# The last four stores behind the If for both paths, and another order of quarter products at the end

## The chip, the cores and the metric

One NeuronCore of one Trainium2 chip runs the kernel; the other cores are idle. The metric is the device time of the core, in microseconds (us). A core has five engines that run beside each other: TensorE (PE, with its weight loads shown as PEld), VectorE (DVE), ScalarE (ACT), GpSimd (POOL) and SyncE (SP, which computes nothing here and issues transfers). Each works through its own list of instructions in order; semaphores tie them together.

## The reference

```python
m, k, n = 4096, 4096, 4096
a = np.random.randn(m, k).astype(np.float32)
b = np.random.randn(k, n).astype(np.float32)
alpha = np.float32(0.01)

def reference(a, b, alpha):
    x = np.matmul(a, b)
    return np.where(x > 0, x, alpha * x)
```

A product of two 4096 x 4096 matrices with a leaky ReLU behind it, in float32.

## The kernel before

The output is cut into regions of 1024 x 1024: group `g` of rows (4) by column block `j` (4). A region is four blocks of 512 x 512, and a block is held as four row tiles `mt` of 128 rows by 512 columns. All inputs are rounded to float16 on the way in. Past the first region a region is computed by seven products of half-size matrices in place of eight, with sums of blocks of A (`s1` to `s4`) and of B made beforehand by VectorE. `product` (line 788) runs a whole product, 128 x 512 per matmul. In the regions of the last groups three of the seven, the fourth, the sixth and the seventh, are themselves split into seven products of quarters: `quarter_product` (line 738) multiplies a 256 x 1024 quarter of the A side by a 1024 x 256 quarter of the B side, in 16 matmuls of 128 x 256 (8 chunks `c` of the depth by 2 row tiles `m`). In it `x[h, k]` and `b[k, n]` are quarters themselves, `sx(n)` are sums of quarters of A that were kept in memory and are loaded again, and `t(n)` are sums of quarters of B.

Each product of quarters enters one or more quarters of the block. With rows `r` (row tiles 0 and 1, or 2 and 3) and columns `n` (left or right 256), the seven enter as follows: `x[0,0] b[0,0]` into all four; `x[0,1] b[1,0]` into (0,0); `sx(2) t(2)` into (0,1), (1,0) and (1,1); `sx(1) t(1)` into (0,1) and (1,1); `sx(4) b[1,1]` into (0,1); `sx(3) b[0,1]` into (1,0) and (1,1); `x[1,1] t(4)` into (1,0).

The last region's seventh product is written out by itself, in `seventh_at_the_end`. Its block already has a part in the PSUM banks `y[0..3]` (one per row tile). The banks `one` and `one_more` (their left halves are `ones`) collect what enters several quarters, the bank `other` holds `sx(1) t(1)`, and `kept[mt]` in SBUF, four tiles of 128 x 512 float32, collects the block. ScalarE copies banks to `kept`, VectorE adds banks to it (`add`, line 949; lines 928, 929 and 940) and applies `leaky` (line 310). With `by_row=True` a product finishes its first row tile before it begins the second. `leave` (line 960) applies `leaky` to a pair of row tiles and issues their stores on SP.

The instructions of this part stand in the order in which they are written: the kernel runs under a manual schedule, and each engine gets its own in that order.

The shortened product holds only for inputs of a certain evenness. Sums over the squares of A and B are collected beside the work; `judge` makes them into one number `good`, and `values_load` reads it into a register `even` of every engine. Behind the last region all engines compare `even`: where it is 1, SP issues the last store (line 1201); where it is not, the `Else` computes everything again in bfloat16 with plain products, 8 row blocks by 8 column blocks, and stores it over the whole output. With the inputs above `even` is 1. At the end of either path each engine brings the semaphore counts that belong to it up to what the other path would have left, and goes to the close of the program (line 1262): SP waits for each DMA counter, and the engines meet twice.

SP's list at the end, in order: four stores of `v_pairs`, four of `u2_pairs`, the load of `even`, the two stores of row tiles 0 and 1 (line 960), the store of row tile 2 (line 944), the branch (line 1200), the store of row tile 3 (line 1201). Each store is 256 KB.

## Time and profile before

| | us |
|---|---|
| median of 3 runs | 1539.24 (1538.66 to 1540.42) |
| the profiled execution, its own time | 1540.23 |
| its span | 1538.1 |
| PE busy in the span | 1524.4 (99%) |
| DVE, ACT, POOL busy | 1158.1, 426.0, 281.9 |
| end of the last matmul, of the last VectorE instruction | 1528.85, 1530.83 |
| issue of the last store | 1530.90 |

The span runs from the first to the last instruction that the profiler recorded, 2.1 us less than the execution's own time. The profile page gives busy time per engine, the chain of work that ended last, groups of instructions, waits and transfers; a line such as L738 is a line of the kernel's source, and a "q" behind an engine's name (SPq) marks an instruction of that engine's sequencer, which issues, waits or branches and leaves the engine's data path idle. A row of a source line gives the operation, its count, its least, median and greatest length in ns, and its first and last start in us. TensorE's granted clock was 0.998 of full speed.

### The profile page before, as it was taken

What the parts mean: (1) busy time and instruction counts of PE and PEld (TensorE: products, weight loads), DVE (VectorE), ACT (ScalarE), POOL (GpSimd) and SP (SyncE); (2) the same over time, 40 slices, a digit from 0 to 9 for tenths busy, and PEclk for the clock granted to TensorE, in tenths of its full rate; (3) what the DMA queues carried; (4) which work ended last, traced back from release to release, by engine and by line L of the source; (5) the groups of instructions that cost most, each with busy time, mean ns of one, the idle gap of its engine ahead of it and who ended that gap; (6) DMA issues with size and microseconds to landing.
All of it is one profiled execution on the core that took longest, in us unless ns stands there. A gap on an engine that the chain in (4) does not pass through costs nothing.

```text
span 1538.1 us, 21821 instructions
## 1 busy us (share of the span) xinstructions
PE 1524.4 (99%) x8667; PEld 846.8 (55%) x8667; DVE 1158.1 (75%) x1201; ACT 426.0 (28%) x730; POOL 281.9 (18%) x458
## 2 busy tenths in 40 slices
PE   9999999999999999999999999999999999999997
PEld 4444444444446567574544747557544475747656
DVE  4368867766699686768769698676977868797496
ACT  2201334647310213103641130312454112041210
POOL 5641110243202011022220202010331110101100
PEclk9999999999999999999999999999999999999999
DMA  9999895998879979599797979969899895948924
GB/s 247 187 212 202 235 282 168 174 192 182 229 277 282 252 174 275 135 291 258 171 290 263 287 183 213 253 160 320 165 245 309 216 282 144 292 164 182 286 99 140
DMA packets 205442, 342.87 MB, mean 223 GB/s; under 512 B 18833, under 2 KB 148113, under 8 KB 195346
## 3 DMA queue, kind: packets, MB, share of 16 engines
q0 software_dynamic: 136704, 129.00, 52.7%
q1 hardware_dynamic: 62002, 186.81, 32.9%
q10 hardware_dynamic: 6624, 25.56, 4.4%
q8 instruction: 70, 1.15, 0.3%
q14 instruction: 42, 0.34, 0.1%
HBM read 361.76 MB, written 106.43 MB: 304 GB/s over the span
## 4 chain that ended last, share of the span: by engine, by line
PE 67%; DVE 1%; issue 0%; DVEq 0%
PE ps L788 45%; PE ps L738 22%; DVE c L310 0%; DVE c L949 0%; DVE c L843 0%; DVE c L940 0%; DVE c L954 0%; DVE b L667 0%; DVEq L940 0%
## 5 line engine op out<-in xcount | busy, mean ns | idle before, releaser
L788 PE MATMUL ps<-b,a 128*128 128x512 f16 x2624 | 570.8, 379 | 0.0
L788 PE MATMUL ps<-b,s 128*128 128x512 f16 x2240 | 489.2, 379 | 0.0
L788 PEld LDWEIGHTS <-a 128*128 128x128 f16 x2624 | 256.6, 98 | 307.9 <-issue 0.3
L788 PEld LDWEIGHTS <-s 128*128 128x128 f16 x2240 | 219.1, 98 | 262.6 <-issue 0.4
L575 DVE TENSOR_TENSOR b<-b 128x4096 f16<-128x4096 f16 x104 | 235.1, 2289 | 65.4 <-DMA b<-in_b_dram 56.7
L519 POOL DMA_DIRECT2D b<-in_b_dram x160 | 118.6, 746 | 866.2 <-PE ps L738 327.6
L801 ACT COPY c<-ps 128x512 f32<-128x512 f32 x164 | 84.6, 596 | 452.1 <-PE ps L788 365.0
L141 DVE STREAM_TRANSPOSE a<-a 128x512 uint32<-128x512 uint32 (+2 forms) x120 | 126.8, 1104 | 96.6 <-DMA a<-in_a_dram 96.6
L132 POOL DMA_DIRECT2D a<-in_a_dram x252 | 137.3, 551 | 264.8 <-ACT junk L594 97.6
L738 PEld LDWEIGHTS <-q 128*128 128x128 f16 x1424 | 139.3, 98 | 16.9 <-issue 0.8
L594 ACT ACTIVATE junk<-a 128x512 bf16<-128x512 f16 x192 | 121.1, 631 | 97.6 <-DMA a<-in_a_dram 92.4
L310 DVE SCALAR_TENSOR_TENSOR c<-c 128x1024 f32<-128x1024 f32 (+1 forms) x121 | 141.5, 1212 | 4.4 <-ACT c L801 4.2
L230 ACT ACTIVATE sq<-b 128x2048 bf16<-128x2048 f16 x64 | 119.1, 1909 | 57.6 <-DVE sq L239 41.8
L738 PEld LDWEIGHTS <-a 128*128 128x128 f16 x1200 | 117.3, 98 | 17.9 <-DVE q L677 0.3
L949 DVE TENSOR_TENSOR c<-ps,c 128x512 f32<-128x512 f32 x142 | 88.8, 683 | 48.0 <-PE ps L788 34.4
L282 PE MATMUL ps<-b,a 128*128 128x512 f16 x512 | 112.8, 379 | 2.1 <-DVE part L321 0.9
L738 PE MATMUL ps<-b,q 128*128 128x256 f16 x784 | 92.1, 273 | 0.6 <-DVE c L843 0.6
L738 PE MATMUL ps<-b,a 128*128 128x256 f16 x752 | 88.3, 273 | 0.0
L282 PEld LDWEIGHTS <-a 128*128 128x128 f16 x512 | 49.7, 98 | 63.1 <-issue 3.2
L890 ACT COPY c<-ps 128x512 f32<-128x512 f32 x9 | 5.3, 586 | 269.9 <-PE ps L738 120.2
L738 PEld LDWEIGHTS <-s 128*128 128x128 f16 x624 | 61.0, 98 | 7.1
L843 DVE TENSOR_TENSOR c<-ps,c 128x512 f32<-128x512 f32 x80 | 52.3, 687 | 13.5 <-PE ps L738 13.5
(104 smaller groups left out, 903.7 us busy)
## 6 DMA issues: line engine op xcount, KB each, us to landing
b<-in_b_dram POOLq DMA_DIRECT2D x168, 512.0 KB, 13.0
out_dram<-c SPq DMA_DIRECT2D x240, 256.0 KB, 5.6
a<-in_a_dram POOLq DMA_DIRECT2D x244, 128.0 KB, 5.6
b<-kept SPq DMA_DIRECT2D x20, 1024.0 KB, 9.1
q<-kept_qs ACTq DMA_DIRECT2D x40, 512.0 KB, 7.7
s<-kept_s SPq DMA_DIRECT2D x18, 1024.0 KB, 7.5
q<-kept_qa SPq DMA_DIRECT2D x28, 512.0 KB, 6.7
b<-kept_last SPq DMA_DIRECT2D x12, 1024.0 KB, 11.5
```

Source lines behind the costliest of these rows:

```text
L132: nc.gpsimd.dma_start(a16[32 * q:32 * q + 32], src.rearrange("(g i) w -> i g w", i=32))
L141: nc.vector.transpose(part.rearrange("p c m e -> p c (m e)").bitcast(U32) .rearrange("p c (g i) -> p g c i", i=32), src[:, :, i * n:(i + 1 ...
L230: nc.scalar.activation(to, self.parts[n], SQUARE)
L282: nc.tensor.matmul(ps, a_cols(at[0, h, u], c, mt, (h, u) == (0, 0)), bt[0, u, nt][:, c, :], start=first, stop=last,)
L310: nc.vector.scalar_tensor_tensor(t, t, alpha, t, op0=MULT, op1=MAX if alpha <= 1 else MIN)
L519: nc.gpsimd.dma_start(t[:, c:c + 4, :], b_rows(j, u, c, 4, nt, g > 0))
L575: nc.vector.tensor_tensor(f(to), f(x0), f(x1), op)
L594: nc.scalar.activation(junk, piece[:, q, :], SQUARE, accum_out=to[:, 4 * n + q:4 * n + q + 1])
L738: nc.tensor.matmul(to[m], xq[:, c // 2, rows, c % 2], yq[:, c, :], start=first and c == 0 and m < banks, stop=c == KC - 1, skip_group_chec ...
L788: nc.tensor.matmul(banks[mt], a_cols(t, c, mt, t is first_a), B(half, nt, k)[:, c, :], start=first and (k, c) == todo[0], stop=(k, c) == t ...
L801: nc.scalar.copy(kept[mt], banks[mt])
L949: nc.vector.tensor_add(to, bank, to)
```

## The change

Two things change. In `seventh_at_the_end` the seven products of quarters stand in another order, the block is finished quarter by quarter, and no store is issued in it: it returns the four pairs of destination and tile. Behind the last region the `If` now holds the fallback alone, with the condition turned round, and has no `Else`; the four stores stand behind it, for both paths. So that they store the right thing on either path, the fallback does not store the four tiles of this block itself: it writes them to a buffer `back` in memory and loads them from there, on POOL's queue, into the tiles `last[mt][1]`, which the stores then write out.

The order of products before: `x[0,0] b[0,0]`, `sx(4) b[1,1]`, `sx(2) t(2)`, `sx(1) t(1)`, `x[0,1] b[1,0]`, `x[1,1] t(4)`, `sx(3) b[0,1]`. After: `x[0,0] b[0,0]`, `x[0,1] b[1,0]`, `sx(2) t(2)`, `sx(1) t(1)`, `sx(4) b[1,1]`, `sx(3) b[0,1]`, `x[1,1] t(4)`, the last two by row. `even` is now loaded behind the second product, before it was behind the fifth.

```diff
+            part = lambda t, n: t[:, n * HALF:(n + 1) * HALF]
+            onto = lambda r, n: [part(y[2 * r + m], n) for m in range(2)]
+            ones = [part(bank, 0) for bank in (one, one_more)]
+
+            def more(mt, n, bank):
+                nc.vector.tensor_add(part(kept[mt], n), bank, part(kept[mt], n))
 
             quarter_product(x[0, 0], b[0, 0], ones, True, banks=2)
-            copies(0)
+            for m in range(2):
+                nc.scalar.copy(part(kept[m], 0), ones[m])
+            for mt in (2, 3):
+                nc.scalar.copy(part(kept[mt], 1), part(y[mt], 1))
+            quarter_product(x[0, 1], b[1, 0], onto(0, 0))
+            for mt in range(2):
+                more(mt, 0, part(y[mt], 0))
+            leaky(block(0, 0))
+            even = nc.values_load(good[0:1, 0:1], min_val=0, max_val=1)
+            quarter_product(sx(2), t(2), ones)
+            for m in range(2):
+                nc.scalar.copy(part(kept[m], 1), ones[m])
+            quarter_product(sx(1), t(1), into(other), True)
+            for r in (1, 0):
+                nc.vector.tensor_add(block(r, 1), pair(other), block(r, 1))
             quarter_product(sx(4), b[1, 1], onto(0, 1))
-            quarter_product(sx(2), t(2), ones)
-            copies(1)
+            for mt in range(2):
+                more(mt, 1, part(y[mt], 1))
+            leaky(block(0, 1))
+            quarter_product(sx(3), b[0, 1], ones, by_row=True)
+            for m in range(2):
+                nc.scalar.copy(part(kept[2 + m], 0), ones[m])
+                more(2 + m, 1, ones[m])
+            leaky(block(1, 1))
+            quarter_product(x[1, 1], t(4), onto(1, 0), by_row=True)
             for mt in (2, 3):
-                nc.scalar.copy(kept[mt][:, HALF:], y[mt][:, HALF:])
-            quarter_product(sx(1), t(1), into(other), True)
-            nc.vector.tensor_add(block(0, 1), pair(other), block(0, 1))
-            nc.vector.tensor_add(block(1, 1), pair(other), block(1, 1))
-            quarter_product(x[0, 1], b[1, 0], onto(0, 0))
-            even = nc.values_load(good[0:1, 0:1], min_val=0, max_val=1)
-            add(kept[:2], y[:2])
-            leave(pairs[:1], 0, 1)
-            quarter_product(x[1, 1], t(4), onto(1, 0))
-            for mt in (2, 3):
-                nc.scalar.copy(kept[mt][:, :HALF], y[mt][:, :HALF])
-            quarter_product(sx(3), b[0, 1], ones, by_row=True)
-            for mt in (2, 3):
-                both_halves = kept[mt].rearrange("p (h n) -> p h n", h=2)
-                nc.vector.tensor_add(both_halves, ones[mt - 2].unsqueeze(1).to_broadcast([P, 2, HALF]), both_halves)
-                leaky(kept[mt])
-                last = place(g, 0, mt, j, 1), kept[mt]
-                if mt == 2:
-                    nc.sync.dma_start(*last)
-            return even, last
+                more(mt, 0, part(y[mt], 0))
+                leaky(part(kept[mt], 0))
+            return even, [(place(g, 0, mt, j, 1), kept[mt]) for mt in range(MT)]
...
-    with tc.If(even == 1) as inputs:
-        nc.sync.dma_start(*last)
-
-    with inputs.Else():
+    back = dram_pool.tile([MT, P, NT], FP32, name="back")
+    about_to_leave = 2 * regions[-1][0], 2 * regions[-1][1] + 1
+    with tc.If(even == 0):
...
-                    nc.sync.dma_start(out[(m * MT + mt) * P:(m * MT + mt + 1) * P, cols], t)
+                    if (m, n) == about_to_leave:
+                        nc.sync.dma_start(back[mt], t)
+                        nc.gpsimd.dma_start(last[mt][1], back[mt])
+                    else:
+                        nc.sync.dma_start(out[(m * MT + mt) * P:(m * MT + mt + 1) * P, cols], t)
+    for to, t in last:
+        nc.sync.dma_start(to, t)
```

More of the change, by code (lines that the diff above doesn't have):

```diff
@@ L912, in seventh_at_the_end @@
             block = lambda r, n: pairs[r][:, :, n * HALF:(n + 1) * HALF]
-            onto = lambda r, n: [y[2 * r + m][:, n * HALF:(n + 1) * HALF] for m in range(2)]
-            ones = [bank[:, :HALF] for bank in (one, one_more)]
-            def copies(n):
-                for m in range(2):
-                    nc.scalar.copy(kept[m][:, n * HALF:(n + 1) * HALF], ones[m])
-            quarter_product(x[0, 0], b[0, 0], ones, True, banks=2)
-            copies(0)
-            quarter_product(sx(4), b[1, 1], onto(0, 1))
```

## The prediction

> **What bounds the kernel now.** I read the page first (shares, then the chain that ended last), next the timeline of the last 35 us, and then the sequencers' own rows of the lines that hold the branch and the close. From the page:

> ```profile
> span 1538.1 us, 21821 instructions
> PE 1524.4 (99%) x8667; PEld 846.8 (55%) x8667; DVE 1158.1 (75%) x1201; ACT 426.0 (28%) x730; POOL 281.9 (18%) x458
> ```

> TensorE is busy for 1524.4 of 1538.1 us, and the change leaves its 8667 matmuls as they are. What can move is what lies around them: 13.7 us, nearly all of it at the end. The chain that ended last, from 1440 us on, in order of time (start, length, what):

> ```profile
> 1504.40 23.59 PE ps L738 x216
> ...
> 1528.08 0.70 DVE c L940
> ...
> 1530.14 0.69 DVE c L310
> ```

> It passes from TensorE to VectorE 0.8 us before the last matmul ends (1526.94 + 1.91 = 1528.85) and stops at 1530.83: 7.3 us of the span come after all arithmetic. The timeline of that end:

> ```profile
> 1526.61 1.23 DVE L310 SCALAR_TENSOR_TENSOR c<-c 128x1024 f32<-128x1024 f32 x1
> 1526.94 1.91 PE L738 MATMUL ps<-b,q 128*128 128x256 f16 x16
> 1528.08 0.69 DVE L940 TENSOR_TENSOR c<-ps,c 128x512 f32<-128x512 f32 x1 [0.25 <-PE ps L738]
> 1528.81 0.69 DVE L310 SCALAR_TENSOR_TENSOR c<-c 128x512 f32<-128x512 f32 x1
> 1529.42 0.68 DVE L940 TENSOR_TENSOR c<-ps,c 128x512 f32<-128x512 f32 x1
> 1529.57 0.33 SPq L944 DMA_DIRECT2D out_dram<-c  x1
> 1530.14 0.69 DVE L310 SCALAR_TENSOR_TENSOR c<-c 128x512 f32<-128x512 f32 x1
> 1530.90 0.33 SPq L1201 DMA_DIRECT2D out_dram<-c  x1
> ```

> Two adds and two leaky ReLUs, each 512 wide, follow the last product one behind the other; the last store is issued 0.07 us later. The other 7.2 us are in the views of line 1200 (the If) and line 1262 (the program's close):

> ```profile
> L1200 SPq EVENT_SEMAPHORE  x7: 17/17/17, 1533.4 to 1533.8; - x7
> L1200 PEldq COMPARE_BRANCH  x2: 90/2090/4089, 1526.7 to 1529.1; - x2
> L1200 SPq COMPARE_BRANCH  x2: 43/46/49, 1529.9 to 1533.9; - x2
> L1200 DVEq COMPARE_BRANCH  x2: 51/53/55, 1530.2 to 1531.0; - x2
> ```

> ```profile
> L1262 SPq EVENT_SEMAPHORE  x14: 17/28/28, 1536.5 to 1538.1; - x14
> ...
> L1262 DVEq DRAIN  x2: 10/34/58, 1534.3 to 1537.6; - x2
> ```

> SP sits still until 1533.4, when row tile 2's store (issued 1529.57, landing 3.8) is in; it then brings seven DMA counters up to what the other path would have left (1533.4 to 1533.9), branches over the fallback at 1533.9, and shows nothing until the first closing wait at 1536.5. None of its closing waits lasts over 0.028 us, so those 2.6 us are no wait for a transfer. VectorE loses 1531.0 to 1534.3 = 3.3 in the same place, PE 4.1, ACT 1527.8 to 1530.2 = 2.4, POOL 1506.6 to 1509.2 = 2.6. I read this as the code of the jump's target coming in: the DMA records show instruction blocks of 8 KB moving at 1534.8 and 1534.9.

> [...]

> **The change, part by part.**

> 1. TensorE: the same seven products of 16 matmuls in another order, 0. In the built order the products wait for nothing that is not there: `sx(2)`, `sx(1)` and `t(2)` keep their slots (third, fourth), `sx(4)` and `t(4)` move later, and `sx(3)`, whose load is issued at 1514.9 (such loads land in 7.7, the median over the run), is used at 1525.4, not 1527.1. New waits: `sx(4)`'s product onto `y[0..1]` waits for VectorE's adds of the left halves, done by 1521.5, two slots before. If this cover failed it would cost what is late, one for one.

> 2. VectorE: nine instructions become fifteen, narrower. Widths: 512 takes 0.69 and 1024 takes 1.22, so 256 takes about 0.42 (an estimate on that line; bounds 0.34, half of 0.69, and 0.69). Independent ones start 0.08 before the one ahead ends, dependent ones 0.03 after. With products ending each 1.745 us up to 1528.85, I walk the queue: left halves of tiles 0 and 1 and their leaky 1520.7 to 1522.2 (the queue is free at 1520.8); the two adds of `other` 1523.65 to 1524.9; right halves of tiles 0, 1 1525.3 to 1526.0, leaky to 1526.8; tile 2 right at 1526.7, tile 3 right at 1527.6 (it stands behind ScalarE's copy, 0.38 from 1527.1), leaky of both to 1528.7; then tile 2 left 1528.6 to 1529.05, leaky to 1529.5; tile 3 left to 1529.85, leaky to 1530.3. So VectorE ends at 1530.3, not 1530.83: 0.5 gained, not the 1.1 that the short last steps alone would give, because the wide leaky of tiles 2 and 3 now stands ahead of them. Bounds 0.2 to 0.9.

> 3. The If: every engine now jumps over the fallback before the stores. SP's comparison moves up to about 1522.9, right behind its load of `even` (issued at 1521.7, the last register step at 1522.8); no store stands before it. Jump 2.5 to 4.1: 1525.4 to 1527.0. At the far side it waits for all eight counters (the stores in flight landed by 1523.8) and raises them, eight steps at 0.07: 1526.0 to 1527.6. Queued behind it are the four stores. Tile 0 and 1 are ready at 1526.8, tile 2 at 1529.5, tile 3 at 1530.3, so the jump on SP costs nothing: 2.7 us or more of slack up to the third store, and up to 4.1 the first two only go out later. The stores also wait for counters that POOL raises; POOL jumps at 1505.4. The adjacent branches behind the jump I take at 0: at the program's start the same kind of branch leaves no row, and 0.07 us separate the instructions on its two sides.

> 4. The tail. Last store issued 1530.35. Its landing: rows give 2.3 to 3.8 near the end (2.0 is the least since 1500); in the run before the last 2 KB packets end by 1533.6, 2.7 after its issue. I take 2.65: 1533.0. Then SP's closing waits: twelve in 1536.5 to 1537.2, 0.06 each; the last store's counter is sixth, six are left, 0.4, drains 0.1, and the handshake of all engines, 1537.3 to 1538.1, 0.8. Sum 1533.0 + 1.3 = 1534.3.

> 5. VectorE's own jump is on the way too: it leaves at 1529.9, as its last leaky is issued; with its own 3.3 it is at its drain at 1533.35, just ahead of SP at 1533.5. With 2.5 it has 0.9 to spare; with PE's 4.1 it sets the end at 1535.0. PE leaves at 1526.8 and is back by 1530.9.

> Sum: 1538.1 - 1534.3 = 3.8 gained: 0.5 from VectorE, 0.5 the counters, 2.6 the jump, 0.3 closing waits passed while the last store is in flight, 0.1 lost between landings. The profiled run took 1540.23, 2.1 around its span; the median of the runs, 1539.24, lies 0.99 lower. I set the difference against the median: **1535.4 us**.

> **Rivals.**

> One, a new wait takes the jump's place: VectorE's fetch takes PE's 4.1 (1535.0), or the last store takes row tile 2's 3.8 (1530.35 + 3.8 + 1.3 = 1535.45), as both now fall into the same microseconds. Gain 2.7 to 3.1: 1536.4. For it: the slow rows are those beside stores. Against: there the last store still took 2.7.

> Two, the gap was no code: SP's 2.6 us come anyway at the close. Left are 0.5 + 0.5 + 0.3 = 1.3: 1537.9. [...] Against: five engines show the gap, each right behind its second branch, POOL 29 us before the end.

> Three, the change does not do what it says: the jump leaves the tail of one engine and is paid several times by another. The path not taken has three branches (into the stub, behind the If, to the close). If each fetches anew, VectorE needs three times 2.5 to 3.3 from 1529.9: 1537.4 to 1539.8, plus drain and handshake 0.9: 1538.3 to 1540.7, middle 1539.5, or **1540.6 us, slower**. It decides once VectorE is back later than 1537.2. Against: the branch at the start without a gap. SP would stand at 1534.8 by 4.0 a hop, and its stores with it, so slower by over 0.2% lies inside this case.

> **How the numbers follow.** Forecast 0.66, rival one 0.16, two 0.08, three 0.08, other 0.02. The likeliest case's range: landing 2.0 to 3.2, VectorE's width and its jump, and half a microsecond of the runs' scatter (1538.66 to 1540.42): 1534.3 to 1536.3. With rival one and the lower edge of two: 1534.2 to 1537.4. 0.2% (3.1 us, to 1536.2 and 1542.3) is about what can be told from no change. Faster: five sixths of the forecast and a third of rival one, 0.60. Slower by that much: a good half of rival three and mishaps, 0.06. Within: the rest, 0.34.

> **What would show it.** SP's branch near 1522.9 and nothing between the last store's issue and its closing wait but the landing; the last leaky 256 wide, ending near 1530.3; the close within 1.5 us of the landing; VectorE's drain before SP's. It is wrong if a gap of 2 us or more stands behind the landing, if TensorE idles between the last seven products, or if VectorE or PE reports after SP.

## The result, and the profile after

| | before | changed |
|---|---|---|
| median, us | 1539.89 (22 runs, 1537.35 to 1544.40) | 1537.31 (22 runs, 1535.30 to 1538.92) |
| span of the profiled execution | 1538.1 | 1535.5 |
| last product ends | 1528.85 | 1528.79 |
| last VectorE instruction ends | 1530.83 | 1530.22 |
| last store issued | 1530.90 | 1530.25 |
| span's end behind the last product | 9.27 | 6.75 |

The ratio of the times is 0.9980, 95% interval 0.9973 to 0.9987: faster by about 3 us (the medians lie 2.6 apart), less than the 3.8 forecast. A second set of 11 runs beside other experiments gave 0.9978 (0.9969 to 0.9987). The last row is the one to compare between profiles. The beginning of the last seven products wanders between 1514.5 and 1516.7 from one profile to the next, in kernels that are the same up to there, and the span wanders with it.

The end of the chain that ended last, in the changed kernel (start, length, what):

```profile
1504.34 22.72 PE ps L738 x208
...
1527.08 0.38 ACT c L943
...
1527.48 0.44 DVE c L919
...
1529.80 0.43 DVE c L310
```

It leaves TensorE at 1527.1, earlier than before: from there a copy on ScalarE and then VectorE's queue, not the last product, set the end of the arithmetic. The rows of the If's line (1209), of the four stores' line (1243, the last line of its view) and of the close (1274):

```profile
L1209 SPq EVENT_SEMAPHORE  x8: 17/17/17, 1525.5 to 1526.1; - x8
...
L1209 SPq COMPARE_BRANCH  x1: 50/50/50, 1522.8 to 1522.8; - x1
L1209 PEldq COMPARE_BRANCH  x1: 3731/3731/3731, 1526.7 to 1526.7; - x1
...
L1209 DVEq EVENT_SEMAPHORE  x1: 21/21/21, 1533.2 to 1533.2; - x1
```

```profile
DMA to landing us min/median/max: 2.4/3.8/3.9
```

```profile
L1274 DVEq DRAIN  x2: 10/14/17, 1533.3 to 1535.0; - x2
```

SP branches at 1522.8, is back after 2.7, and has raised its counters by 1526.1, before the first tile is ready. TensorE's jump takes 3.7 from 1526.7, VectorE's 3.4 from 1529.8; both report before SP. Behind the last landing no jump is left. The landings in the line of 1243 are those of the first three stores (3.8, 3.9 and 2.4); that of the last is not among them. The new length is in SP's waits, from 1520 us on (who waited for what, sum, times, longest):

```profile
SPq L1274 <- DMA out_dram<-c: 3.3, 2, 2.3
...
SPq L1209 <- SPq L1209: 2.7, 1, 2.7
```

SP now waits 2.3 us for the last store alone. That store was issued at 1530.25, and SP's wait for its counter ends at 1534.22: 3.97, where the sum had 2.65.

### The profile page after: what moved, and what is told of

The parts are those of the page before. It is cut to its first block, busy times and chain, and to the rows that moved or that the text cites. A ratio compares the mean times of both kernels' runs of the same rounds, so it can differ in the third digit from the quotient of the medians.

```text
span 1535.5 us, 21822 instructions
## 1 busy us (share of the span) xinstructions
PE 1523.8 (99%) x8667; PEld 846.9 (55%) x8667; DVE 1158.7 (75%) x1207; ACT 426.2 (28%) x730; POOL 281.9 (18%) x458
## 3 DMA queue, kind: packets, MB, share of 16 engines
q8 instruction: 70, 1.15, 0.3%
## 5 line engine op out<-in xcount | busy, mean ns | idle before, releaser
L738 PEld LDWEIGHTS <-q 128*128 128x128 f16 x1424 | 139.3, 98 | 16.2
L310 DVE SCALAR_TENSOR_TENSOR c<-c 128x1024 f32<-128x1024 f32 (+2 forms) x123 | 141.5, 1190 | 4.5 <-ACT c L801 4.2
L738 PEld LDWEIGHTS <-a 128*128 128x128 f16 x1200 | 117.4, 98 | 18.4 <-DVE q L677 0.8
L738 PE MATMUL ps<-b,q 128*128 128x256 f16 x784 | 91.8, 273 | 0.0
L738 PE MATMUL ps<-b,a 128*128 128x256 f16 x752 | 88.3, 273 | 0.0
L738 PEld LDWEIGHTS <-s 128*128 128x128 f16 x624 | 61.1, 98 | 7.0
```

The source lines that it names most:

```text
L310: nc.vector.scalar_tensor_tensor(t, t, alpha, t, op0=MULT, op1=MAX if alpha <= 1 else MIN)
L738: nc.tensor.matmul(to[m], xq[:, c // 2, rows, c % 2], yq[:, c, :], start=first and c == 0 and m < banks, stop=c == KC - 1, skip_group_chec ...
```

## Experiments

Two theories of the 3.97 were on record. A: TensorE's jump makes its next 16 KB block of code come in, on one of the 16 DMA engines (in the records of the changed kernel it is one packet, 1531.18 to 1532.74), and the last store's share on that engine waits behind it. B: a store so close behind another takes 4.0 from its issue, whatever else moves. "Tail" below is the span's end behind the last product; "landing", where no other store is named, is from the last store's issue to the end of SP's closing wait for its counter. All ratios are to the kernel before, in runs on the same chip.

**Each part alone.** The stores behind the If, with the products in the order of before:

```diff
+    with tc.If(even == 0):
+        ...
+    for to, t in last:
+        nc.sync.dma_start(to, t)
```

> The stores behind the If as in the changed kernel, the products in the order of before. Both theories: SP's branch at 1522.8 and no gap behind the last landing, VectorE ends at 1530.8 and the last store is issued at 1530.9, so the If alone brings most of the gain. They part at the landing. Theory A (TensorE's jump fetches its next block of code at 1531.2, 16 KB for 1.6 us on one DMA engine, and the last store's share on that engine waits behind it): the landing is tied to the block and not to the issue, 1534.2 to 1534.5 as in the changed kernel, span 1535.5 to 1535.8. Theory B (a store so close behind another takes 4.0 from its issue, whatever else moves): landing 1534.9, span 1536.2.

Measured: 0.9979 (0.9970 to 0.9988), tail 6.57, VectorE 1.98 behind the last product as before, landing 3.19. Against the last product the counter's wait ends at 5.25; A had 5.35 to 5.65 there (1534.2 to 1534.5 with that product's end at 1528.85), B 6.05: 0.1 under A and 0.8 under B. The If alone is worth what the whole change is.

The new order of products with the If and Else of before:

```diff
             leaky(block(0, 1))
+            for mt in range(2):
+                nc.sync.dma_start(place(g, 0, mt, j, 1), kept[mt])
...
+    with tc.If(even == 1) as inputs:
+        nc.sync.dma_start(*last)
+    with inputs.Else():
```

> The new order of products with the If and Else of before: the store of row tile 3 in the If, SP's jump behind it. Both theories: VectorE ends at 1530.2, SP's gap of 2.6 us stays behind its seven counters. If the order is worth its 0.5 by itself, the span is 1537.4 to 1537.6. If the landing of row tile 2's store sets the counters and is held by TensorE's code block (theory A), it is worth less than 0.3: 1537.8 to 1538.1, unless that store now passes before the block, then up to 1.5: 1536.6.

Measured: 0.9997 (0.9988 to 1.0006), tail 8.76, SP's jump 2.6 behind the counters as before. The tail is 0.5 shorter, but the times can't tell that from nothing, and the profile doesn't credit it to VectorE's shorter queue: the counters wait for row tile 2's store, and that landed 1.49 behind the end of a 16 KB block in both kernels (before: block from 1530.27 to 1531.91, landing at 1533.40; here: 1528.74 to 1530.06, 1531.55). Against the last product the block ended 0.55 earlier here, which accounts for the difference.

**Without the jumps.** The If and the fallback taken out:

```diff
-    back = dram_pool.tile([MT, P, NT], FP32, name="back")
-    with tc.If(even == 0):
-        ...
     for to, t in last:
         nc.sync.dma_start(to, t)
```

> The changed kernel without the If and the fallback in it (so without the second computation in bfloat16), the four stores straight behind the last product. No engine jumps. Theory A: no code block of TensorE's jump is in the way, the last store lands 2.0 to 2.7 after its issue at 1530.25, and the close is at 1533.6 to 1534.2. Theory B: it still takes 4.0, the close stays at 1535.5.

Measured: 0.9971 (0.9960 to 0.9982), tail 4.80, landing 2.05.

The If kept, its target brought near:

```diff
-        for m in range(M // RM):
+        for m in range(1):
...
-            for n in range(N // NT):
+            for n in range(1):
```

> The changed kernel with a fallback cut to its first row block and its first column block (the other 63 blocks of the fallback are left out). The If and the branches stay, and their target is near. If the gaps are code coming in, SP, VectorE, ScalarE and POOL show less than 0.3 us behind their branch, VectorE reports by 1530.6, and by theory A the last store lands within 2.7, close at 1533.6 to 1534.2. If the gap belongs to the branch whatever its distance, 2.4 to 3.3 stay on every engine and the close is at 1535.5.

Measured: 0.9968 (0.9956 to 0.9980), tail 5.00, landing 2.22. The rows of the If's line in its profile:

```profile
L1209 SPq EVENT_SEMAPHORE  x4: 17/17/17, 1523.3 to 1523.5; - x4
...
L1209 SPq COMPARE_BRANCH  x1: 50/50/50, 1523.1 to 1523.1; - x1
L1209 PEldq COMPARE_BRANCH  x1: 1477/1477/1477, 1527.0 to 1527.0; - x1
...
L1209 DVEq COMPARE_BRANCH  x1: 72/72/72, 1530.1 to 1530.1; - x1
L1209 DVEq EVENT_SEMAPHORE  x1: 21/21/21, 1530.5 to 1530.5; - x1
```

SP's 2.7 has become 0.2. VectorE's 3.4 has become 0.4, all of it its own last leaky (to 1530.5), and ScalarE and POOL show 0.4 and 0.5, above the 0.3 that was expected; on ScalarE that is its own last copy, on POOL it stays open. TensorE's row is down from 3.7 to 1.5. The branches are still there, the distance is gone, and no 8 KB block of code moves between 1507.0 and 1535.0. So the gaps were code coming in from afar, and without them the last store lands 1.75 to 1.9 sooner: the tails of these two are 4.5 and 4.3 shorter than before, and the times agree (0.0029 and 0.0032 of 1540 are 4.5 and 4.9).

**Moving TensorE's block.** Matmuls of zeros behind the last product, so that TensorE branches later:

```diff
+            spare = new_bank(zbank)
+            for _ in range(6):
+                nc.tensor.matmul(spare, w[:, :P], w, start=True, stop=True)
```

> The changed kernel with six more matmuls (128 x 512 of zeros into a bank that nothing reads) behind the last product, 1.3 us on TensorE, so that it branches at 1528.0 and not 1526.7 (times as in the changed kernel's profile, last product ending 1528.8). Nothing that the output needs is touched. Theory A: the second code block moves from 1531.2 to 1532.5, behind the last store's packets; the last store lands 2.1 to 2.7 after its issue and not 4.0, and the end comes at 5.0 to 5.6 after the last product, set by VectorE's return from its jump, not 6.75. Theory B (4.0 from its issue, or the stores in each other's way): no change, 6.75.

Measured: 0.9977 (0.9966 to 0.9987), tail 5.55 (A had 5.0 to 5.6, B 6.75), landing 2.76 (A had 2.1 to 2.7). TensorE's branch came 0.65 later against the last product, not 1.3, since its sequencer met the branch 2.75 ahead of the end of its last matmul, in the changed kernel 2.1; its first block then ended 0.2 behind the last store's issue, and its second began at 1531.54, behind that store's last packet (1531.43).

With 24 in place of 6, a single run:

> The same with 24 such matmuls, 5.2 us: TensorE branches at 1531.9, and no code block of its jump moves before 1533. Theory A: the last store lands 2.1 to 2.5 after its issue; the end is then TensorE's own return, 1531.9 + 3.7 + 0.9 = 1536.5, later than in the changed kernel. Theory B: the landing stays at 4.0.

Measured: TensorE branched 1.15 behind the last product (3.1 had been expected), 4.0 ahead of the end of its last matmul; its first block fell into the last store, at 1531.19, where the changed kernel has its second at 1531.18. Landing 3.69. As a test of "no block" it failed; as one of "another block in the same place" it speaks for A.

With 48, a single run:

> The changed kernel with 48 zero matmuls behind the last product, so that TensorE branches some 6 us after the last product ends (24 of them moved it by 3.2 and not 5.2, since it reads ahead; its block fell into the last store again). No 16 KB block of the jump moves while the last store is in flight, VectorE's 8 KB blocks still do. Theory A: the landing is 2.1 to 2.9 from the issue at 1.43 behind the last product; the end is late, by TensorE's return. Theory B: 4.0.

Measured: TensorE's branch at 1534.2, landing 2.79. The end is TensorE's return, tail 11.5. The movement of the DMA engines shows the difference. First the changed kernel, from 1530.2 to 1534.2 in 40 slices of 0.1 us (mean busy share of the 16 engines in tenths; queue 8 carries TensorE's code, since its blocks move with TensorE's branch, from 1531.18 here to 1535.29 with 48 matmuls; queue 14 carries that of the other engines, the first of its 8 KB blocks behind SP's branch of 1522.8 at 1523.94):

```profile
DMA  3899999749978998111012100101010010030000
...
q1 hardware_dynamic: 294, 0.53, 38.3%
q8 instruction: 1, 0.02, 2.4%
q14 instruction: 3, 0.02, 1.8%
```

Then the kernel with 48 matmuls, from 1529.3 to 1532.2 (slices of 0.07), and last the one without the If, from 1528.7 to 1530.8 (slices of 0.05, no code on the way):

```profile
DMA  0599799999836799798998321001101100000000
...
q1 hardware_dynamic: 288, 0.52, 50.5%
q14 instruction: 2, 0.02, 1.7%
```

```profile
DMA  0769979979798953469799999698963000000000
```

In all three the two last stores keep the engines busy. In the changed kernel that is over at 1531.8, and then about one in sixteen goes on for two us more; the records don't name engines, but one that carried the block (to 1532.74) and then its share of the store fits. With 8 KB blocks alone such a tail is 0.7 long, and without code there is none. The last store's counter says the same. It is raised in sixteen steps. Without code in the way all sixteen come within 0.2 us (1530.57 to 1530.76). With 48 matmuls, where two 8 KB blocks move, fourteen are in by 1531.39 and two come at 1532.09 and 1532.15. In the changed kernel, where two 8 KB blocks and one of 16 KB move, thirteen are in by 1532.37, two come at 1533.01 and 1533.09, and the last at 1534.21: as many late steps as blocks (the repeat below has four late steps beside three blocks). That the latest is the share behind the 16 KB block is not recorded, but fits.

The changed kernel once more:

> The changed kernel as it is, a second profile and times beside the next run. Theory A: the last store lands 1.4 to 1.5 behind the end of the 16 KB code block that moves while it is in flight, as in the three profiles so far where there was one (changed kernel, stores alone, TensorE latest: 1.45 to 1.50), whatever its time from the issue; tail 6.4 to 6.9. Theory B (4.0 from the issue): landing 4.0, wherever the block lies.

Measured: landing 4.38, tail 7.16 (above A's 6.4 to 6.9, since the block ended later), 0.9978. This profile is of the slowest of its eleven runs (1538.17; the median is 1536.40). The landing against the 16 KB block that began 0.7 to 1.1 us behind the last store's issue:

| kernel | block starts, takes | landing from issue | counter's wait ends behind the block |
|---|---|---|---|
| changed | 1531.18, 1.56 | 3.97 | 1.48 |
| changed, again | 1531.50, 1.75 | 4.38 | 1.50 |
| stores alone | 1529.68, 0.99 | 3.19 | 1.50 |
| 24 zero matmuls | 1531.19, 1.28 | 3.69 | 1.45 |

From the issue the landing differs by 1.2, from the block's end by 0.05. That, with 2.05 and 2.22 where no code moves (but for the end of a block in the first 0.15 us) and 2.79 where only 8 KB blocks do, decides for A; B falls. The first of the four stores, which has none close ahead of it, shows it too: it landed in 3.76 and 3.99 in the two profiles of the changed kernel, where the block from 1527.8 met it, and in 2.09, 2.26 and 2.23 without the If, with 24 and with 48 matmuls, where none did.

**A shorter queue on VectorE.** The right halves of row tiles 2 and 3 one by one:

```diff
             for m in range(2):
-                nc.scalar.copy(part(kept[2 + m], 0), ones[m])
                 more(2 + m, 1, ones[m])
-            leaky(block(1, 1))
+                leaky(part(kept[2 + m], 1))
+                nc.scalar.copy(part(kept[2 + m], 0), ones[m])
```

> The changed kernel with the right halves of row tiles 2 and 3 taken through VectorE one by one (add, leaky, 256 wide each) ahead of ScalarE's copies, so that the wide leaky no longer stands before the last two tiles. Both theories: VectorE ends 0.4 earlier, 1.0 behind the last product in place of 1.43. Theory A: the landing is tied to the code block of 1531.2, which does not move, and to how much of the last store has passed before it: tail between 5.7 (all passed) and 6.75 (none). Theory B: the landing moves with the issue, tail 6.35.

Measured: 0.9974 (0.9964 to 0.9984), VectorE 1.09 behind the last product (1.43 in the changed kernel), landing 2.89, tail 5.62, below even A's range. The shorter queue did not do that: issuing row tile 2's store took 0.97 in place of 0.33, so the last store was issued 1.40 behind the last product, hardly earlier than in the changed kernel (1.46). The fetches ran late in this profile; the second block came at 1530.92, 2.1 behind the last store's issue and only 0.8 ahead of its landing.

> The two edits together, the last leaky 0.4 earlier and TensorE leaving 1.3 later. Theory A: last store issued 1.0 behind the last product, landing 2.1 to 2.7 later, and the end by VectorE's return (0.6 + 3.3 + 0.1 + 0.8) or the landing (1.0 + 2.4 + 1.25): 4.7 to 5.0 behind the last product, so 1.8 to 2.0 better than the changed kernel, ratio to before 0.9965 to 0.997. Theory B: 6.35, 0.9977.

Measured, with six zero matmuls as well: tail 5.27, landing 2.82, above A's 4.7 to 5.0 and 2.1 to 2.7 but far from B's 6.35; 0.9978 (0.9966 to 0.9990). One of the seven runs took 1540.40, the others 1534.3 to 1535.6, so the ratio decides neither for A's 0.9965 to 0.997 nor for B's 0.9977.

> The kernel with the right halves taken one by one, again, beside the changed kernel on the same chip. If its last store keeps ahead of the second block, as in its first profile (landing 2.9, tail 5.6), its time is 0.9 to 1.2 below the changed kernel's; if that was chance, the tail is 6.2 to 6.4 and the time 0.3 to 0.5 below.

Measured: landing 2.89 and tail 5.32, so that the store keeps ahead of the block again; the time is 0.9986 (0.9977 to 0.9995), median 1536.34 beside 1536.40 for the changed kernel in the same runs. No gain in time is shown, although the two profiles differ by 1.84 us at the end. These two profiles are no fair pair: this one is of the fastest of its eleven runs (1535.06), that of the changed kernel of its slowest (1538.17). What the ends of the other runs look like, and whether a gain is lost in their scatter of some 3 us, stays open. I know of no version with the whole fallback that is shown to beat the changed kernel.

## Why the prediction was right, and where it was wrong

The measured median, 1537.31, lies in the wide range, 0.1 below its upper edge, and the direction was right. It lies outside the 1534.3 to 1536.3 of the likeliest case, and the gain forecast (3.8) was half as large again as the one in the profile (2.6). So the mechanism was right and one term was mis-sized; that the number still fell inside is owed to the room left for rival one. Of the 1.9 by which 1535.4 missed, 0.65 is the time before (1539.89 over 22 runs, 1539.24 over the three on hand), and the landing's 1.3 is the rest. At 0.9980 the gain sits on the 0.2% that the prediction took as its mark, so that neither the 0.60 nor the 0.34 is borne out clearly.

1. *TensorE, 0.* Right: the last seven products take 12.39 us in both profiles.
2. *VectorE, 0.5 by a walk through its queue.* Right: 256 wide takes 0.418 and 0.426 (0.42 had been interpolated), and the end is 1.43 behind the last product (1.45 forecast, 1.98 before). The wide leaky of tiles 2 and 3 does stand ahead of the last tiles. What the 0.5 is worth in time is another matter, see below.
3. *The jump on SP, 2.6, moved off the tail.* Right to 0.1 us in each row, and the short fallback shows that it is code: the compare-and-branch on SP is a row of 0.05 in both, and what follows it goes with the distance, 2.7 to the far target and 0.2 to the near one, where no 8 KB block moves.
4. *"Its landing [...] I take 2.65."* This is the step that failed: 3.97. The term was wrong twice. The 2.65 was read off the last packets of data, but the counter comes later: in the profiles of this study SP's wait ends 0.37 to 0.53 behind the last 2 KB packet. The store of before (last packet 1533.56) raised its counter for the last time at 1534.01, 3.1 behind its issue. And the range 2.0 to 3.8 was taken as scatter, where it has a cause: the step counted each engine's jump as time of that engine and left out the transfer that each jump issues. TensorE compares at the same moment as before (1526.7), but now takes its far branch at once, 2.4 earlier (before: 1529.1). Of the two blocks that it fetches behind it, the first met the stores before (1530.27 to 1531.91; row tile 2's 3.8 was such a meeting), and now the second (1531.18 to 1532.74) meets the last one.
5. *VectorE's own jump.* Right: back at 1533.2, drained at 1533.3 (1533.35 forecast), and it would be the bound if the last store landed in 2.65.

Rival one came nearest in mechanism: with the last store taking row tile 2's 3.8 it put the end of the span at 1535.45, measured 1535.5. It had only the general reason that things fall together, and what was held against it, that the last store of before took 2.7, was the reading off the packets. (In time, rival two's 1537.9 lies nearer to the median, but only because the time before was set too low.) Rival two is refuted by the near target, rival three by the changed profile, where no row of a branch stands behind the jump and VectorE, back at 1533.2, is at its drain 0.1 later. In the sum, 0.5 from VectorE was counted on top of the rest. The stores alone (tail 6.57, with VectorE's end as late as before) and the order alone (0.9997) show no such gain; that it is given back at the landing, since an earlier issue doesn't move the block that the landing hangs on, is argued from A.

## What to carry to other kernels

Put a far branch where the engine that takes it has time to spare, ahead of its last wait and not behind it; here that was worth 2.7 of 1540 us in the profile with no change to the arithmetic (the stores alone). Count for such a jump both the time on its engine (2.4 to 3.4 here, on TensorE a row of 3.4 to 4.5) and the blocks that it fetches: here a last store behind whose issue a 16 KB block began 0.7 to 1.1 later landed in 3.2 to 4.4, one with no code on the way in 2.05. Take a transfer's end from its counter, not from its last packet (here SP's wait ended 0.37 to 0.53 later), and price a store that must be the last one with what else moves at that moment.
